# A two-layer hybrid diffusion transformer on one core: the tensor engine keeps the written order of its products and transposes

## The chip, the core and the metric

The kernel runs on one core of a Trainium2 chip. Its time is that of one execution on the device, in microseconds (us). A core has five engines, each with a queue of its own that it works through in order: PE (matrix products and transposes; its loads of stationary operands are shown apart as PEld), DVE (vectors), ACT (scalar functions and copies), POOL (general) and SP, which here only issues DMAs. Products go to PSUM, which is used in eight banks; everything else is in the on-chip memory SBUF.

## The reference

Two layers over 512 tokens (256 of a context, 256 latent), width 1024. All arithmetic is fp32. Per layer, with modulation vectors m that are linear in SiLU of a condition:

```python
h  = rms_norm(x, g) * (1 + scale) + shift            # adaln, per token
x += 0.5 * gate1 * (silu(h @ w_gate) * (h @ w_up)) @ w_down
h  = adaln(x)
x += gate2 * (sum_b sigmoid(h @ G_b + b_b) * (y_b(h) @ w_branch[b])) @ w_out
x += 0.5 * gate3 * swiglu(adaln(x))                   # as in line 2, other weights
```

The four branches y_b of the middle step, the mixer, are a gated short convolution, window attention with a sink, a recurrence run in both directions (RG-LRU), and attention over a neighbourhood on a grid. Context tokens read only context; latent tokens read both. The second layer's mixer and second feed-forward half are needed for the latent tokens alone. The output is the latent stream.

## The kernel before

**Tiling.** The stream lives transposed in eight tiles `x[c]` of 128 features by 512 tokens (columns 0 to 255 context, 256 to 511 latent). An fp32 product is made of three products (`mm3`, L189): high part by high part, high by low, low by high. Weights come from HBM by SP's DMAs (`fetch`, `take`), ACT copies the high part (L150) and DVE subtracts to get the low one (L151). One `mm3` term with 256 columns is three instructions of 0.12 us each on PE.

**Banks.** `BANKS` (L54) gives three PSUM banks to tag A, two to B, one each to C, D and E, eight in all. A tile of a tag takes the bank that was given out longest ago, and its first writer must wait until the last reader of that bank's earlier tile is done.

**A stage and its seam.** A feed-forward half (`ffn`, L420) makes 22 gate and up pairs, then eight tiles of the down product. A tile of the down product, or of the mixer's last product, is added to `x[c]` by DVE (`residual`, L396, the instruction is L399). The last two tiles, c = 6 in bank A and c = 7 in bank B, are made for the context tokens first and then for the latent ones (`finish_stream`, L387). Meanwhile the norm of the next stage is made for the context: squares (ACT), their sum over features on PE (`norm_sum`, L318), then `norm_chain` (L323): DVE scales to `ms` (L326), PE transposes it into bank C (L329), POOL takes the power (L333), PE spreads the result over 128 rows (L337, into D for the context and E for the latent tokens), and `norm_apply` (L343) writes h for eight tiles with two DVE instructions (L351, L353) and one ACT instruction each. So the next stage begins on context tokens while the latent half of the last one is still being added. In the mixer the start is L773 to L788: for each of eight k, one term each of two token-major tiles `T` (bank B), then of two feature-major tiles `F` (bank A). In `ffn` it is L443 to L449: for each k, gate and up terms of two pairs (banks A, B, A, B). There are four such seams:

- M1: first feed-forward half to mixer, layer 0 (at 405 us)
- F1: mixer to second feed-forward half, layer 0 (at 844 us)
- F2: layer 0 to layer 1 (at 1212 us)
- M2: first feed-forward half to mixer, layer 1 (at 1579 us)

**What sets the order.** The program is written in one order, in which a small planner (`later`, `spend`, `until`, L167 to L178) sets side work (norm sums, transposes of heads, gates of the recurrence, attention) between the terms of the big products by a running clock. The framework's scheduler then builds each engine's queue from this program; before the change it lets a ready instruction go ahead of one written earlier when its own model of the times says so. In the mixers the heads are transposed by `flip` (L582: PE L585 into bank E, then an ACT copy L586 out of it), which shares the single bank E with the gates of the recurrence (`gate`, L715: PE L719, ACT L720). `turn` (L644) transposes attention weights in bank C. At the program's start `first_tiles` (L373) interleaves modulation sets (`mod_set`, L259), the first norm, and the first gate and up terms.

Of the kernel before, what the change touches and what calls it, by code (L numbers as in the profile page):

```python
# [35 lines left out]
class Net:  # L36
    def __init__(self, nc, tc, a, out, ctx):
        self.nc, self.tc, self.a, self.out = nc, tc, a, out
        self.n = 0
        pool = lambda name, bufs, **k: ctx.enter_context(tc.tile_pool(name=name, bufs=bufs, **k))  # L40
        self.cp = pool("cst", 1)
        self.hp = pool("h", 16)
        self.wp = pool("w", 3)
        self.whp = pool("wh", 4)
        self.bp = pool("b", 1)
        self.sp = pool("small", 2)
        self.pp = pool("psum", 1, space=PSUM)
# [139 lines left out]


    def mm3(self, ps, wh, wl, xh, xl, first, last):  # L189
        mm = self.nc.tensor.matmul  # L190
        mm(ps, wh, xh, start=first, stop=False)  # L191
        mm(ps, wh, xl, start=False, stop=False)  # L192
        mm(ps, wl, xh, start=False, stop=last)  # L193
# [65 lines left out]
    def mod_set(self, l, s):  # L259
        nc = self.nc  # L260
        ps = self.ps("D", (128, 128))
        for k in range(KC):
            w = self.first[s, k][:].rearrange("p (g n) -> p g n", g=4)
            for g in range(4):
                nc.tensor.matmul(ps[32 * g:32 * g + 32, :], self.sc[:, k, :], w[:, g, :], start=(k == 0),  # L265
                                 stop=(k == KC - 1), tile_position=(0, 32 * g))
        sb = self.half()[:, 0:128]
        nc.scalar.activation(sb, ps, AF.Copy)
        pt = self.ps("E", (128, 4, 32))
        nc.tensor.transpose(pt[:].rearrange("p g n -> p (g n)"), sb, self.ident)  # L270
        bm = self.par[l][:, O_BM + 4 * s:O_BM + 4 * s + 4]
        nc.vector.tensor_tensor(self.mods[l][:, s], pt[:, :, 0:2], bm.unsqueeze(2).to_broadcast([128, 4, 2]), op=ALU.add)
        self.derive(l, s)
# [11 lines left out]
    def norm_stat(self, n, c, s):  # L285
        nc = self.nc
        if c == 0:
            n["ps"][s] = self.ps("DE"[s], (64, 128))
        sq = self.half()
        nc.scalar.activation(sq, self.x[c][:, 256 * s:256 * s + 256], AF.Square)  # L290
        for t in range(2):
            nc.tensor.matmul(n["ps"][s][32 * t:32 * t + 32, :], self.ones, sq[:, 128 * t:128 * t + 128],
                             start=(c == 0), stop=(c == KC - 1), tile_position=(0, 32 * t))

    def norm_square(self, n, c, s):
# [15 lines left out]
    def norm_sum(self, n, s, c, sq):  # L311
        nc = self.nc
        if c == 6:
            n["ps"][s] = self.ps("DE"[s], (64, 128))
        for t in range(2):
            w = slice(128 * t, 128 * t + 128)
            for p, v in enumerate((n["acc"][s], sq) if c == 6 else (sq,)):
                nc.tensor.matmul(n["ps"][s][32 * t:32 * t + 32, :], self.ones, v[:, w], start=(c == 6 and p == 0),  # L318
                                 stop=(c == 7), tile_position=(0, 32 * t))
        if c == 7:  # L320
            self.job(self.norm_chain(n, s), (n["l"], n["i"], s))

    def norm_chain(self, n, s, R=None):  # L323
        nc = self.nc
        ms = self.small((64, 128), "ms", 2)
        nc.vector.tensor_scalar(ms, n["ps"][s], 1.0 / D, EPS, op0=ALU.mult, op1=ALU.add)  # L326
        yield 500
        pt = self.ps("C" if R is None else "A", (128, 2, 32))
        nc.tensor.transpose(pt[:].rearrange("p g n -> p (g n)"), ms, self.ident[:64, :64])  # L329
        v = self.small((128, 2), "v4")  # L330
        nc.vector.tensor_copy(v, pt[:, :, 0])
        r = self.small((128, 2), "r4")
        nc.gpsimd.tensor_tensor(r, v, self.mhalf.to_broadcast([128, 2]), op=ALU.pow)  # L333
        yield 2500 if s else 1900
        n["R"][s] = self.ps("DE"[s], (128, 256)) if R is None else R
        for t in range(2):
            nc.tensor.matmul(n["R"][s][:, 128 * t:128 * t + 128], r[:, t:t + 1].to_broadcast([128, 128]), self.ident,  # L337
                             start=True, stop=True)
        if R is None:
            for c in range(KC):  # L340
                self.norm_apply(n, c, s)
# [225 lines left out]
    def heads(self, ps, t, nh, gain, dst, rot, tag):  # L567
        nc = self.nc
        w = 64 * nh
        q = self.blk(tag, (128, 256))  # L570
        nc.scalar.activation(q[:, :w], ps[:, :w], AF.Copy)
        sq = self.half()
# [4 lines left out]
        r = self.small((128, 4), "rs")  # L577
# [4 lines left out]
        def flip(x, out):  # L582
            pt = self.ps("E", (128, 2, 128))
            for p in range(np_):
                nc.tensor.transpose(pt[:, p], x[:, 128 * p:128 * p + 128], self.ident)  # L585
            nc.scalar.activation(out, pt[:, :np_], AF.Copy)  # L586
            self.pending -= 1

# [55 lines left out]
    def turn(self, p, nk):  # L644
        nc = self.nc
        pt = self.ps("C", (128, 4, 128))
        for j in range(nk // 128):
            nc.tensor.transpose(pt[:, j], p[:, 128 * j:128 * j + 128], self.ident)  # L648
        pT = self.blk("a", (128, 4, 128))
        nc.scalar.activation(pT[:, :nk // 128], pt[:, :nk // 128], AF.Copy)  # L650
        return pT

    def attend(self, step, segs, out, keys, queries, value, biases, sink):


        nc = self.nc
        U = [(pr, sg, qb) for pr in range(2) for sg in segs for qb in range(2)]
        P, T, Y, bias = {}, {}, {}, {}
        nk = lambda u: 512 if u[1] else 256

        def scores(u):
            pr, sg, qb = u
            qw = slice(128 * qb, 128 * qb + 128)
            S = [self.ps("B"), self.ps("B")]
            for j in range(nk(u) // 256):
                for hh in range(2):
                    rows = slice(64 * hh, 64 * hh + 64)
                    nc.tensor.matmul(S[hh][:, 256 * j:256 * j + 256], queries(sg, j)[rows, pr, qw], keys(j, pr)[rows],  # L668
                                     start=True, stop=True)
            P[u] = self.softmax(S, nk(u), (lambda hh: bias[pr](hh, qb)) if sg else None, lambda hh: sink(pr, hh))  # L670
            if pr == 0 and u == U[len(U) // 2 - 1]:
                bias[1] = biases(1)

        def values(u):
            pr, sg, qb = u
            if qb == 0:
                Y[pr, sg] = self.ps("D", (128, 256))
            y = Y[pr, sg]
            n = nk(u) // 128
            for j in range(n):  # L680
                for hh in range(2):
                    nc.tensor.matmul(y[64 * hh:64 * hh + 64, 128 * qb:128 * qb + 128], value(j, pr, hh), T[u, hh][:, j],  # L682
                                     start=(j == 0), stop=(j == n - 1), tile_position=(0, 64 * hh))
            if qb == 1:
                if len(out) == pr:
                    out.append(self.blk("ya"))
                nc.scalar.activation(out[pr][:, 256 * sg:256 * sg + 256], y, AF.Copy)

        bias[0] = biases(0)
        while self.pending:  # L690
            yield 300
        for i in range(len(U) + 2):
            a, b, c = (U[i - d] if 0 <= i - d < len(U) else None for d in range(3))
            if c:
                values(c)
                yield step
            if b:
                T[b, 0] = self.turn(P[b][0], nk(b))
                yield step
            if a:  # L700
                scores(a)
                yield 2 * step
            if b:
                T[b, 1] = self.turn(P.pop(b)[1], nk(b))
            yield 2 * step

    def recurrence(self, segs, out, U, bd, sp2, hb, step):
        nc = self.nc
        S3 = lambda x: x[:].rearrange("p (s t) -> p s t", s=2)
        for c in range(2):  # L710
            for d in range(2):
                k = 2 * d + c
                u = U[c] if d == 0 else U[c][:, ::-1, :]

                def gate(j, g):  # L715
                    pz = self.ps("E")
                    for s in range(2):
                        src = s if d == 0 else 1 - s
                        nc.tensor.matmul(pz[:, 256 * s:256 * s + 256], bd[:, 4 * j + k], U[c][:, src], start=True, stop=True)  # L719
                    nc.scalar.activation(g, pz, AF.Tanh, scale=0.5, bias=hb[:, 4 * j + k:4 * j + k + 1])  # L720

                t, q, b = (self.blk("r") for _ in range(3))
# [7 lines left out]
                w = self.blk("t")  # L730
# [305 lines left out]
```

## Time and profile before

| | |
|---|---|
| median of three runs | 2041.42 us (2040.87 to 2042.23) |
| profiled execution: time, span | 2040.34 us, 2038.6 us |
| PE busy | 2010.8 us, 99% of the span |
| DVE busy, ACT busy | 1331.3 us (65%), 800.3 us (39%) |
| granted clock of PE over the span | 0.997 |
| DMA | 145 GB/s, 41.4% of its engines' time |

An engine's idle time costs only where the chain that ended last runs through it. A row of the timeline gives start, length and, in square brackets, how long the engine had been idle before and what released it. PE's records overlap (a product's record is 0.28 long while the next begins 0.12 later), so the distance of the starts is what a product takes.

### The profile page before, as it was taken

How to read it: one execution, taken by the hardware profiler on the slowest of the kernel's cores; microseconds unless marked ns; L12 is line 12 of the kernel's file. 1: busy time of each engine (PE TensorE's matmuls, PEld its weight loads, DVE VectorE, ACT ScalarE, POOL GpSimd, SP SyncE). 2: the span in 40 equal slices, each digit the busy share in tenths (PEclk: the TensorE clock that was granted, in tenths of full speed). 3: DMA queues.
4: the chain of work that ended last, by engine and by line, in shares of the span. 5: the costliest groups of instructions: out<-in, count | busy, mean ns of one | idle time of the engine just before them, and what ended most of it. 6: DMA issues, size and time to landing. Idle time of an engine off the chain costs nothing.

```text
span 2038.6 us, 29838 instructions
## 1 busy us (share of the span) xinstructions
PE 2010.8 (99%) x11765; PEld 1732.7 (85%) x11765; DVE 1331.3 (65%) x2914; ACT 800.3 (39%) x1311; POOL 87.3 (4%) x90
## 2 busy tenths in 40 slices
PE   7999999999999999999999999999999999999999
PEld 4888887897797788888888888888888999999999
DVE  4878986667555545685733358689844788775554
ACT  3332232356444434232222333222323676664443
POOL 0000000120010000100000010000002101010000
PEclk9999999999999999999999999999999999999999
DMA  9554653522222224244532233446434324463453
GB/s 350 167 212 172 223 207 125 180 68 60 70 91 76 78 94 154 83 166 152 186 106 90 72 139 145 173 168 237 179 125 131 86 91 136 152 231 141 169 191 121
DMA packets 61549, 295.50 MB, mean 145 GB/s; under 512 B 14689, under 2 KB 16353, under 8 KB 38241
## 3 DMA queue, kind: packets, MB, share of 16 engines
q1 hardware_dynamic: 61408, 293.60, 41.4%
q8 instruction: 92, 1.51, 0.3%
q14 instruction: 49, 0.39, 0.1%
HBM read 292.53 MB, written 1.05 MB: 144 GB/s over the span
## 4 chain that ended last, share of the span: by engine, by line
PE 93%; DVE 3%; issue 2%; DMA 1%; ACT 1%; POOL 0%; SPq 0%; POOLq 0%; ACTq 0%; DVEq 0%
PE A L191 19%; PE A L192 18%; PE A L193 18%; PE B L191 11%; PE B L192 11%; PE B L193 11%; DVE a L249 1%; PE B L668 1%; PE D L682 1%; PE C L648 1%; PE E L719 1%; DVE wl L151 1%; DMA w<-in_dn 0%; ACT wh L150 0%; PE D L265 0%
## 5 line engine op out<-in xcount | busy, mean ns | idle before, releaser
L150 ACT ACTIVATE wh<-w 128x1024 fp32r<-128x1024 f32 (+2 forms) x476 | 428.1, 905 | 863.7 <-PE A L192 333.5
L151 DVE TENSOR_TENSOR wl<-w,wh 128x1024 fp32r<-128x1024 f32 (+2 forms) x476 | 490.1, 1033 | 286.5 <-ACT wh L150 283.6
L191 PE MATMUL A<-h,wh 128*128 128x512 f32 (+1 forms) x1440 | 506.9, 352 | 5.8 <-ACT wh L150 3.3
L193 PE MATMUL A<-h,wl 128*128 128x512 f32 (+1 forms) x1440 | 496.2, 345 | 1.2 <-DVE wl L151 1.1
L192 PE MATMUL A<-h,wh 128*128 128x512 f32 (+1 forms) x1440 | 496.3, 345 | 0.7 <-DVE h L353 0.7
L249 DVE CUSTOM_DVE_ANT_0 a<-w,rows 128x512 f32<-128x512 f32 x512 | 350.4, 695 | 41.1 <-DMA w<-in_mod 32.3
L191 PEld LDWEIGHTS A<-h,wh 128*128 128x128 f32 x1440 | 273.2, 190 | 48.3 <-issue 11.5
L193 PEld LDWEIGHTS A<-h,wl 128*128 128x128 f32 x1440 | 273.4, 190 | 35.1 <-DVE wl L151 2.5
L192 PEld LDWEIGHTS A<-h,wh 128*128 128x128 f32 x1440 | 273.5, 190 | 31.8 <-DVE h L353 1.4
L191 PE MATMUL B<-h,wh 128*128 128x512 f32 (+1 forms) x736 | 262.2, 356 | 0.0
L193 PE MATMUL B<-h,wl 128*128 128x512 f32 (+1 forms) x736 | 261.7, 356 | 0.0
L192 PE MATMUL B<-h,wh 128*128 128x512 f32 (+1 forms) x736 | 261.7, 356 | 0.0
L191 PEld LDWEIGHTS B<-h,wh 128*128 128x128 f32 x736 | 139.8, 190 | 19.9 <-ACT wh L150 0.4
L192 PEld LDWEIGHTS B<-h,wh 128*128 128x128 f32 x736 | 139.7, 190 | 19.6 <-issue 0.4
L193 PEld LDWEIGHTS B<-h,wl 128*128 128x128 f32 x736 | 139.6, 190 | 19.6
L432 DVE TENSOR_TENSOR t<-t,B 128x512 f32<-128x512 f32 (+1 forms) x88 | 54.2, 619 | 107.4 <-PE B L193 106.4
L307 POOL TENSOR_TENSOR nb<-nb,l 128x256 f32<-128x256 f32 x45 | 47.2, 1066 | 1320.0 <-ACT l L305 1320.0
L191 PE MATMUL A<-b,wh 128*128 128x512 f32 (+1 forms) x246 | 85.4, 347 | 1.0 <-ACT wh L150 1.0
L193 PE MATMUL A<-b,wl 128*128 128x512 f32 (+1 forms) x246 | 85.1, 346 | 1.1 <-DVE wl L151 1.1
L192 PE MATMUL A<-b,wh 128*128 128x512 f32 (+1 forms) x246 | 84.9, 345 | 0.0
L191 PE MATMUL B<-b,wh 128*128 128x512 f32 (+1 forms) x204 | 73.1, 358 | 0.4 <-ACT wh L150 0.4
L193 PE MATMUL B<-b,wl 128*128 128x512 f32 (+1 forms) x204 | 73.1, 358 | 0.3 <-DVE wl L151 0.3
(266 smaller groups left out, 2927.4 us busy)
## 6 DMA issues: line engine op xcount, KB each, us to landing
w<-in_gu SPq DMA_DIRECT2D x88, 1024.0 KB, 4.9
w<-in_mod SPq DMA_DIRECT2D x64, 1024.0 KB, 4.8
w<-in_dn SPq DMA_DIRECT2D x64, 704.0 KB, 4.1
w<-in_gb SPq DMA_DIRECT2D x64, 640.0 KB, 3.8
w<-in_fm SPq DMA_DIRECT2D x10, 1024.0 KB, 4.8
w<-in_tm SPq DMA_DIRECT2D x10, 1024.0 KB, 5.0
w<-in_wo SPq DMA_DIRECT2D x8, 1024.0 KB, 4.8
b<-in_first SPq DMA_DIRECT2D x20, 256.0 KB, 6.2
```

The lines of the kernel that those rows point to most:

```text
L150: nc.scalar.activation(hi[i][:, :e], t[:, o:o + e], AF.Copy)
L151: nc.vector.tensor_tensor(lo[i][:, :e], t[:, o:o + e], hi[i][:, :e].bitcast(F32), op=ALU.subtract)
L191: mm(ps, wh, xh, start=first, stop=False)
L192: mm(ps, wh, xl, start=False, stop=False)
L193: mm(ps, wl, xh, start=False, stop=last)
L249: nc.vector.tensor_tensor_reduce(out=junk, in0=w[:, g, k], in1=self.rows[:, v, k], scale=1.0, scalar=0.0, op0=ALU.mult, op1=ALU.add, accum ...
L307: nc.gpsimd.tensor_tensor(n["acc"][s], n["acc"][s], sq, op=ALU.add)
L432: nc.vector.tensor_tensor(s[:, lo:hi], s[:, lo:hi], ps[1][:, lo:hi], op=ALU.mult)
L648: nc.tensor.transpose(pt[:, j], p[:, 128 * j:128 * j + 128], self.ident)
L668: nc.tensor.matmul(S[hh][:, 256 * j:256 * j + 256], queries(sg, j)[rows, pr, qw], keys(j, pr)[rows], start=True, stop=True)
L682: nc.tensor.matmul(y[64 * hh:64 * hh + 64, 128 * qb:128 * qb + 128], value(j, pr, hh), T[u, hh][:, j], start=(j == 0), stop=(j == n - 1), ...
L719: nc.tensor.matmul(pz[:, 256 * s:256 * s + 256], bd[:, 4 * j + k], U[c][:, src], start=True, stop=True)
```

## The change

`Net` gets an object `pe` whose `matmul` and `transpose` issue the same instruction and mark it to be kept in the program's order on its engine: no wait is added to the instruction, but the scheduler may no longer let another instruction of PE go ahead of it. All of PE's issues go through it (`mm3`, `mod_set`, `norm_stat`, `norm_sum`, `norm_chain`, `flip`, `turn`, both products in `attend`, `gate`). Shown are the addition and two of the ten places; the others read alike.

```diff
     def __init__(self, nc, tc, a, out, ctx):
         self.nc, self.tc, self.a, self.out = nc, tc, a, out
+        mm, tr = nc.tensor.matmul, nc.tensor.transpose
+        class PEq:
+            pass
+        self.pe = PEq()
+        self.pe.matmul = lambda *a, **k: tc.keep_in_program_order(mm(*a, **k))
+        self.pe.transpose = lambda *a, **k: tc.keep_in_program_order(tr(*a, **k))
...
     def mm3(self, ps, wh, wl, xh, xl, first, last):
-        mm = self.nc.tensor.matmul
+        mm = self.pe.matmul
...
             for p in range(np_):
-                nc.tensor.transpose(pt[:, p], x[:, 128 * p:128 * p + 128], self.ident)
+                self.pe.transpose(pt[:, p], x[:, 128 * p:128 * p + 128], self.ident)
```

The instructions are the same ones. 525 of PE's 11,257 stand in another place, by at most 50 places; so do 176 of DVE's and 36 of ACT's, none of POOL's. All of PE's have the line of one of the two lambdas now (L43 products, L44 transposes), and all later lines of the file move by six (L399 becomes L405).

PE at seam M1, before; B_3365 and B_3366 are the two token-major tiles `T`, A_3363 and A_3364 the feature-major ones, h_294, h_296 the high parts of h for k = 0, 1:

```order
L191 MATMUL B_3365<-wh_3079,h_294 128x256
L192 MATMUL B_3365<-wl_3081,h_294 128x256
L193 MATMUL B_3365<-wh_3079,h_295 128x256
L191 MATMUL A_3363<-h_294,wh_3069 128x256
L192 MATMUL A_3363<-h_295,wh_3069 128x256
L193 MATMUL A_3363<-h_294,wl_3071 128x256
L191 MATMUL A_3364<-h_294,wh_3070 128x256
L192 MATMUL A_3364<-h_295,wh_3070 128x256
L193 MATMUL A_3364<-h_294,wl_3072 128x256
L191 MATMUL B_3365<-wh_3079,h_296 128x256
```

And now:

```order
L43 MATMUL B_3365<-wh_3079,h_294 128x256
L43 MATMUL B_3365<-wl_3081,h_294 128x256
L43 MATMUL B_3365<-wh_3079,h_295 128x256
L43 MATMUL B_3366<-wh_3079,h_294 128x256
L43 MATMUL B_3366<-wl_3081,h_294 128x256
L43 MATMUL B_3366<-wh_3079,h_295 128x256
L43 MATMUL A_3363<-h_294,wh_3069 128x256
L43 MATMUL A_3363<-h_295,wh_3069 128x256
L43 MATMUL A_3363<-h_294,wl_3071 128x256
L43 MATMUL A_3364<-h_294,wh_3070 128x256
L43 MATMUL A_3364<-h_295,wh_3070 128x256
L43 MATMUL A_3364<-h_294,wl_3072 128x256
```

The terms of the second token-major tile B_3366 stood 31 rows after the first row shown; now its first three stand right behind the first three of B_3365, and the products of k = 0 in bank A behind them.

DVE at the same seam, before: the last applications of the context's norm, and between them the residual of the latent half of tile 7 (x_94 from B_3088, the tile whose bank B_3366 takes next):

```order
L351 SCALAR_TENSOR_TENSOR l_3242<-x_93,A_83,D_3215 128x256
L353 SCALAR_TENSOR_TENSOR h_303<-l_3234,mods_81,h_302 128x256
L351 SCALAR_TENSOR_TENSOR l_3246<-x_94,A_83,D_3215 128x256
L353 SCALAR_TENSOR_TENSOR h_305<-l_3238,mods_81,h_304 128x256
L399 SCALAR_TENSOR_TENSOR x_94<-B_3088,G_85,x_94 128x256
L353 SCALAR_TENSOR_TENSOR h_307<-l_3242,mods_81,h_306 128x256
L555 TENSOR_TENSOR nb_4011<-nr_4003,cst 128x256
```

And now:

```order
L357 SCALAR_TENSOR_TENSOR l_3242<-x_93,A_83,D_3215 128x256
L359 SCALAR_TENSOR_TENSOR h_303<-l_3234,mods_81,h_302 128x256
L357 SCALAR_TENSOR_TENSOR l_3246<-x_94,A_83,D_3215 128x256
L359 SCALAR_TENSOR_TENSOR h_305<-l_3238,mods_81,h_304 128x256
L405 SCALAR_TENSOR_TENSOR x_94<-B_3088,G_85,x_94 128x256
L359 SCALAR_TENSOR_TENSOR h_307<-l_3242,mods_81,h_306 128x256
L561 TENSOR_TENSOR nb_4011<-nr_4003,cst 128x256
```

On DVE nothing moved here: the residual has the same place behind the same instructions.

PE at seam F1, before; A_7372, B_7373 are gate and up of the first pair, A_7374, B_7375 of the second:

```order
L191 MATMUL A_7372<-h_3288,wh_7095 128x256
L191 MATMUL B_7373<-h_3288,wh_7096 128x256
L191 MATMUL A_7374<-h_3288,wh_7171 128x256
L192 MATMUL A_7372<-h_3289,wh_7095 128x256
L193 MATMUL A_7372<-h_3288,wl_7097 128x256
L192 MATMUL B_7373<-h_3289,wh_7096 128x256
L193 MATMUL B_7373<-h_3288,wl_7098 128x256
L192 MATMUL A_7374<-h_3289,wh_7171 128x256
L193 MATMUL A_7374<-h_3288,wl_7173 128x256
```

And now:

```order
L43 MATMUL A_7372<-h_3288,wh_7095 128x256
L43 MATMUL A_7372<-h_3289,wh_7095 128x256
L43 MATMUL A_7372<-h_3288,wl_7097 128x256
L43 MATMUL B_7373<-h_3288,wh_7096 128x256
L43 MATMUL B_7373<-h_3289,wh_7096 128x256
L43 MATMUL B_7373<-h_3288,wl_7098 128x256
L43 MATMUL A_7374<-h_3288,wh_7171 128x256
L43 MATMUL A_7374<-h_3289,wh_7171 128x256
L43 MATMUL A_7374<-h_3288,wl_7173 128x256
L43 MATMUL B_7375<-h_3288,wh_7172 128x256
L43 MATMUL B_7375<-h_3289,wh_7172 128x256
L43 MATMUL B_7375<-h_3288,wl_7174 128x256
```

B_7375 stood 43 rows behind the first row shown (and the low-part products behind the high-part ones); now it is the fourth tile to begin.

PE in layer 0's mixer, before; E_3771 is a gate of the recurrence, E_3781 and E_3788 are flips, A_3753 a token-major tile:

```order
L719 MATMUL E_3771<-b_3345,bd_3304 128x256 x2
L191 MATMUL A_3753<-wh_3356,h_304 128x256
L192 MATMUL A_3753<-wl_3358,h_304 128x256
L193 MATMUL A_3753<-wh_3356,h_305 128x256
L191 MATMUL A_3753<-wh_3356,h_306 128x256
L192 MATMUL A_3753<-wl_3358,h_306 128x256
L193 MATMUL A_3753<-wh_3356,h_307 128x256
L191 MATMUL A_3753<-wh_3356,h_308 128x256
L585 MATMUL E_3781<-cst,m_3634 128x128 x2
```

And now:

```order
L43 MATMUL E_3771<-b_3345,bd_3304 128x256 x2
L43 MATMUL A_3753<-wh_3356,h_304 128x256
L43 MATMUL A_3753<-wl_3358,h_304 128x256
L43 MATMUL A_3753<-wh_3356,h_305 128x256
L44 MATMUL E_3781<-cst,m_3634 128x128 x2
L43 MATMUL A_3753<-wh_3356,h_306 128x256
L43 MATMUL A_3753<-wl_3358,h_306 128x256
L43 MATMUL A_3753<-wh_3356,h_307 128x256
L44 MATMUL E_3788<-cst,m_3643 128x128 x2
```

The flip E_3781 comes four products earlier, and E_3788, which stood 21 rows further on, follows three products behind it. The same piece stands in layer 1's mixer with other numbers.

## Rows read from the trace of the kernel before

**Rows 1.** The page: busy time of each engine; the chain's shares by engine.
```profile
PE 2010.8 (99%) x11765; PEld 1732.7 (85%) x11765; DVE 1331.3 (65%) x2914; ACT 800.3 (39%) x1311; POOL 87.3 (4%) x90
...
PE 93%; DVE 3%; issue 2%; DMA 1%; ACT 1%; POOL 0%; SPq 0%; POOLq 0%; ACTq 0%; DVEq 0%
```
**Rows 2.** PE's waits: line, what for, total us, times, longest us.
```profile
PE E L337 <- POOL r L333: 2.5, 5, 1.0
PE A L191 <- ACT h L352: 2.3, 2, 1.2
PE A L193 <- DVE wl L151: 2.1, 4, 0.8
...
PE E L270 <- ACT l L268: 0.9, 2, 0.5
```
**Rows 3.** Timeline of PE, 832 to 835: start, length, instruction, idle before.
```profile
834.07 0.30 PE L318 MATMUL D<-l,ones 128*32 128x128 f32 x1 [1.71 <-ACT l L305]
...
834.63 0.39 PE L191 MATMUL B<-b,ya 128*128 128x256 f32 x1
```
**Rows 4.** Timeline of PE and DVE at seam M1.
```profile
405.75 0.28 PE L191 MATMUL A<-h,wh 128*128 128x256 f32 x1
...
407.98 0.47 DVE L399 SCALAR_TENSOR_TENSOR x<-B,G,x 128x256 f32<-128x256 f32 x1
```
**Rows 5.** Timeline of PE and DVE at seam F1.
```profile
844.93 0.39 PE L192 MATMUL A<-h,wh 128*128 128x256 f32 x1
845.15 0.28 PE L193 MATMUL A<-h,wl 128*128 128x256 f32 x1
...
848.73 0.48 DVE L399 SCALAR_TENSOR_TENSOR x<-B,G,x 128x256 f32<-128x256 f32 x1
...
851.30 0.67 DVE L249 CUSTOM_DVE_ANT_0 a<-w,rows 128x512 f32<-128x512 f32 x1
```
**Rows 6.** Timeline of PE and DVE at seam F2.
```profile
1212.85 0.28 PE L191 MATMUL A<-h,wh 128*128 128x256 f32 x1
...
1214.49 0.47 DVE L399 SCALAR_TENSOR_TENSOR x<-B,G,x 128x256 f32<-128x256 f32 x1
```
**Rows 7.** Timeline of PE and DVE at seam M2.
```profile
1579.22 0.28 PE L191 MATMUL A<-h,wh 128*128 128x256 f32 x1
...
1581.44 0.48 DVE L399 SCALAR_TENSOR_TENSOR x<-B,G,x 128x256 f32<-128x256 f32 x1
```
**Rows 8.** Timeline of ACT and PE in layer 0's mixer.
```profile
440.52 0.69 ACT L720 ACTIVATE r<-E,lr 128x512 f32<-128x512 f32 x1 [1.96 <-PE E L719]
440.67 0.28 PE L191 MATMUL A<-wh,h 128*128 128x256 f32 x1
441.22 1.28 ACT L726 ACT_TABLE_LOAD   x1
441.26 0.44 PE L585 MATMUL E<-cst,m 128*128 128x128 f32 x2
443.24 0.36 ACT L586 ACTIVATE b<-E 128x256 f32<-128x256 f32 x1
450.79 0.41 PE L585 MATMUL E<-cst,m 128*128 128x128 f32 x2 [0.61 <-DVE m L593]
```
**Rows 9.** Timeline of ACT in layer 1's mixer.
```profile
1613.98 0.69 ACT L720 ACTIVATE r<-E,lr 128x512 f32<-128x512 f32 x1 [1.29 <-PE E L719]
...
1616.70 0.36 ACT L586 ACTIVATE b<-E 128x256 f32<-128x256 f32 x1
```
**Rows 10.** Timeline of DVE in layer 0's attention.
```profile
464.92 0.61 DVE L641 TENSOR_SCALAR a<-a,mx 128x256 f32<-128x256 f32 x2
```
**Rows 11.** Windows: stretch, length, each engine's busy time (instructions), clock, DMA share, GB/s.
```profile
832.00:836.00 4.00, 2.29 (x20) 1.83 (x20) 2.10 (x5) 0.42 (x1) 0.55 (x1) 1.00 0.80 289
1838.40:1843.50 5.10, 1.47 (x10) 0.80 (x9) 1.94 (x6) 0.92 (x3) 0.71 (x1) 0.97 0.02 6
1843.50:1847.00 3.50, 3.44 (x17) 3.44 (x18) 3.50 (x10) 2.40 (x7) 0.00 (x0) 0.55 0.00 0
1847.00:1851.00 4.00, 4.00 (x35) 4.00 (x35) 1.87 (x5) 0.95 (x2) 0.00 (x0) 1.00 0.00 0
```

More of the change, by code (lines that the diff above doesn't have):

```diff
@@ L264, in mod_set @@
             for g in range(4):
-                nc.tensor.matmul(ps[32 * g:32 * g + 32, :], self.sc[:, k, :], w[:, g, :], start=(k == 0),
+                self.pe.matmul(ps[32 * g:32 * g + 32, :], self.sc[:, k, :], w[:, g, :], start=(k == 0),
                                  stop=(k == KC - 1), tile_position=(0, 32 * g))
@@ L269, in mod_set @@
         pt = self.ps("E", (128, 4, 32))
-        nc.tensor.transpose(pt[:].rearrange("p g n -> p (g n)"), sb, self.ident)
+        self.pe.transpose(pt[:].rearrange("p g n -> p (g n)"), sb, self.ident)
         bm = self.par[l][:, O_BM + 4 * s:O_BM + 4 * s + 4]
@@ L291, in norm_stat @@
         for t in range(2):
-            nc.tensor.matmul(n["ps"][s][32 * t:32 * t + 32, :], self.ones, sq[:, 128 * t:128 * t + 128],
+            self.pe.matmul(n["ps"][s][32 * t:32 * t + 32, :], self.ones, sq[:, 128 * t:128 * t + 128],
                              start=(c == 0), stop=(c == KC - 1), tile_position=(0, 32 * t))
@@ L317, in norm_sum @@
             for p, v in enumerate((n["acc"][s], sq) if c == 6 else (sq,)):
-                nc.tensor.matmul(n["ps"][s][32 * t:32 * t + 32, :], self.ones, v[:, w], start=(c == 6 and p == 0),
+                self.pe.matmul(n["ps"][s][32 * t:32 * t + 32, :], self.ones, v[:, w], start=(c == 6 and p == 0),
                                  stop=(c == 7), tile_position=(0, 32 * t))
@@ L328, in norm_chain @@
         pt = self.ps("C" if R is None else "A", (128, 2, 32))
-        nc.tensor.transpose(pt[:].rearrange("p g n -> p (g n)"), ms, self.ident[:64, :64])
+        self.pe.transpose(pt[:].rearrange("p g n -> p (g n)"), ms, self.ident[:64, :64])
         v = self.small((128, 2), "v4")
@@ L336, in norm_chain @@
         for t in range(2):
-            nc.tensor.matmul(n["R"][s][:, 128 * t:128 * t + 128], r[:, t:t + 1].to_broadcast([128, 128]), self.ident,
+            self.pe.matmul(n["R"][s][:, 128 * t:128 * t + 128], r[:, t:t + 1].to_broadcast([128, 128]), self.ident,
                              start=True, stop=True)
@@ L647, in turn @@
         for j in range(nk // 128):
-            nc.tensor.transpose(pt[:, j], p[:, 128 * j:128 * j + 128], self.ident)
+            self.pe.transpose(pt[:, j], p[:, 128 * j:128 * j + 128], self.ident)
         pT = self.blk("a", (128, 4, 128))
@@ L667, in scores @@
                     rows = slice(64 * hh, 64 * hh + 64)
-                    nc.tensor.matmul(S[hh][:, 256 * j:256 * j + 256], queries(sg, j)[rows, pr, qw], keys(j, pr)[rows],
+                    self.pe.matmul(S[hh][:, 256 * j:256 * j + 256], queries(sg, j)[rows, pr, qw], keys(j, pr)[rows],
                                      start=True, stop=True)
@@ L681, in values @@
                 for hh in range(2):
-                    nc.tensor.matmul(y[64 * hh:64 * hh + 64, 128 * qb:128 * qb + 128], value(j, pr, hh), T[u, hh][:, j],
+                    self.pe.matmul(y[64 * hh:64 * hh + 64, 128 * qb:128 * qb + 128], value(j, pr, hh), T[u, hh][:, j],
                                      start=(j == 0), stop=(j == n - 1), tile_position=(0, 64 * hh))
@@ L718, in gate @@
                         src = s if d == 0 else 1 - s
-                        nc.tensor.matmul(pz[:, 256 * s:256 * s + 256], bd[:, 4 * j + k], U[c][:, src], start=True, stop=True)
+                        self.pe.matmul(pz[:, 256 * s:256 * s + 256], bd[:, 4 * j + k], U[c][:, src], start=True, stop=True)
                     nc.scalar.activation(g, pz, AF.Tanh, scale=0.5, bias=hb[:, 4 * j + k:4 * j + k + 1])
```

## Prediction

> **What bounds the kernel now.** I read the page's busy times and chain first: PE is busy 99% of the span, and 93% of the chain that ended last runs through it [rows 1]. So neither bandwidth nor another engine sets the time; it is the sum of PE's products plus the little that PE stands still. The busy figure leaves 2038.6 − 2010.8 = 27.8 us, some 12 of it before the first product. The work on PE is the same after the change, product for product, so the question is only what idle time a new order adds to these 28 us or takes from them. The list of PE's waits shows what there is to take: in the running part single waits of at most a few tenths each [rows 2]. Then I compared the old and new order of PE and, wherever an instruction comes earlier, asked of the timeline when the thing it needs is there. Where it is ready before PE arrives, the move costs nothing; where not, everything behind it stands, since PE has nothing else in its queue that could go ahead. That this is so, the trace shows: PE stood 1.71 us for one square sum (L318) while the product that came right behind, L191 into B, had all its data [rows 3].
>
> **The four seams.** At M1 the first three products of B_3366 now stand right after those of B_3365. PE reached that place at 405.75 [rows 4]: the product that starts there is the one which stood next in the old order. The bank of B_3366 is that of tile 7 of the down product, of which DVE has yet to read the latent half. On DVE the residual stands behind the context's norm applications and has not moved; it starts at 407.98 and lasts 0.47 [rows 4]. A hand-over from another engine to PE took 0.05 (ACT's copy of 440.52 + 0.69 ends at 441.21, the transpose that waited for it starts at 441.26) [rows 8]. So PE starts B_3366 at 408.50 and stands 408.50 − 405.75 = 2.75. Before, 31 other instructions stood between and hid it.
>
> At F1 the second product of all needs a low part that DVE delivers for 844.93; the third follows at 845.15 [rows 5], and six more come at 0.12 each, so that the tenth, the first of B_7375, is due at 845.15 + 7 × 0.12 = 845.99. The residual ends at 848.73 + 0.48 = 849.21 [rows 5], with the hand-over 849.26: a wait of 3.27. At F2 the fourth tile is due at 1212.85 and free at 1214.49 + 0.47 + 0.05 = 1215.01: 2.16 [rows 6]. At M2 it is 1579.22 against 1581.44 + 0.48 + 0.05 = 1581.97: 2.75 [rows 7]. The four make 10.93.
>
> Behind each of these waits the context's chain goes on without PE, so that the latent norm is helped: the waits of L337 for POOL's power (2.5 in 5, of which 1.0 is in the start [rows 2]) go, −1.5. F1 pays twice more: two products that filled the gap before 844.93 come later (2 × 0.12 = 0.24), and one more background product of DVE, 0.67 long and followed by a short read [rows 5], gets ahead of `ms`; it costs between 0 and 0.75, and I take 0.55, since DVE is idle for some tenths there. Seams: 10.93 + 0.8 − 1.5 = 10.2. What else waits behind: nothing on DVE or ACT is short of time, as they run 65% and 39% [rows 1].
>
> **The flips.** E_3781 comes four products earlier, at 440.67, right behind three products that follow a gate in the same bank. ACT has read the gate at 441.21, so the flip still starts at 441.26 [rows 8]: 0.59 that four products used to fill. E_3788 then follows three products behind it, at about 441.26 + 0.27 + 3 × 0.12 = 441.89, and needs bank E back. The copy that frees it stands on ACT behind a table load of 1.28 and an exponential; it starts at 443.24 and ends at 443.60 [rows 8]. With 0.05 for the hand-over, 443.65 − 441.89 = 1.76. Since the heads go on earlier, the wait of 0.61 at 450.79 [rows 8] goes. Layer 1 has the same piece, with the copy 2.72 after the gate's reading starts in both (443.24 − 440.52, 1616.70 − 1613.98) [rows 8, 9]: 0.59 + 1.76 again, and there no later wait to save. Flips: 2 × 2.35 − 0.61 = 4.1.
>
> **Single moves.** Some six more instructions (turns of attention weights in both layers, the start of the last stage on latent tokens alone) come a few products earlier than their data. Each is then ended by one DVE or ACT instruction under way, at most 0.6 long [rows 10]: between 0 and 3.6, and I take half, 1.8.
>
> **The start.** Up to 61 us the order changes most, but there PE waits for weights and h anyway. The two waits for h (2.3) may go [rows 2]; against that, the transposes of the modulation sets wait 0.45 each for ACT's copy in two of four steps, and with nothing let in between they do in all four, 2 × 0.45 = +0.9 [rows 2]. Bounds −2.3 and +0.9; I take −1.0, a little below the middle, as the next sets no longer break into the gate and up products.
>
> **The clock.** A stall has a second price if it lowers PE's clock. In the trace 1.71 us of standing did not: the granted clock of 832 to 836 is 1.00 (2.4 GHz). A stretch of 5.10 us with 1.47 of work did: the 3.5 us behind it ran at 0.55, near the lower level of 1.2 GHz, with 17 products in 3.44, against 35 in 4.00 after that [rows 11]. Such a fall costs 3.44 − 17 × 4.00 / 35 = 1.5. The new stalls of 2.2 to 3.3 lie between the two cases; I take one fall for the four, 1.5, with bounds 0 and 6.0.
>
> **Sum.** 10.2 + 4.1 + 1.8 − 1.0 + 1.5 = 16.6 on the profiled execution's 2040.34: 2056.9. The median shown is 1.1 above that execution, so 2058.
>
> **The rivals.** First, *the clock falls at all four seams*: 3 × 1.5 more, 2062.5. For it speaks the 1838 stretch, against it that PE is full up to each stall and from its end on. The Trainium skill ("TensorE: Matmul & The Clock Gate", Part 1: The HAM clock gate) has it that the array drops to half rate once it has been idle and comes back only after a spell of sustained work; by that rule this would be the case to expect for the longest stalls, and the 832 window disagrees only for one that is shorter. Chance 0.15.
>
> Second, on the other side, *the residual doesn't hold the bank*: the new tile lands in the bank of tile 5's, read long before (two banks of B are given out in turn, so this turns on one tile more or less), or PE lets the ready products past. Then the seams cost nothing and the savings stay, and the flips, whose copies come in a stream, shrink to the singles: 2041.4 − 1.5 − 0.6 − 1.0 + 1.8 = 2040, not slower. It decides from the point that the residual ends before 405.75, 2.7 us earlier than it does. Against it: the residual is the tile's last reader and stands right there in DVE's queue [rows 4], and PE did not let a ready product past [rows 3]. Chance 0.08.
>
> Third, *part is given back later*: an engine that has been ahead catches up less work later, so that some of PE's old waits vanish, for low parts of weights (2.1 [rows 2]) and for square sums such as the 1.71 [rows 3], with a few singles absent, together about 6 us: 2052. Against it: those waits are set by DMAs and by products just before them, which a late PE delays too. Chance 0.07.
>
> **How the numbers follow.** Forecast 0.70, rivals 0.15, 0.08, 0.07. The lower bounds of the sum (F1's 0.55, singles and clock 0, start −2.3) give 2058 − 0.55 − 1.8 − 1.5 − 1.3 = 2053, the third rival reaches a little lower, so the range begins at 2050; the upper ones (singles +1.8, start +1.9, clock +4.5) give 2066, where it ends. About what a measurement of this kernel can tell from no change is 0.2%, 4.1 us: the forecast and the first and third rivals are slower by more, 0.92; the second lies mostly within it, 0.06, and 0.02 is left for faster.
>
> **What would show it.** Right: four waits of PE on DVE's residual (now L405) of 2 to 3.3 us at 405, 845, 1212 and 1580 (plus what has been added before), two of 1.8 us on ACT's copy out of E in the mixers, the four waits at the latent L337 gone, PE's idle time up from 28 to about 43 us and its busy time unchanged but for the clock. Wrong: no row of PE waiting for a residual; a clock of 1.00 through all seams (the term of 1.5 falls) or about 0.5 behind each (the first rival); an idle time that is far above 45 us.

## The result, and the profile after

The changed kernel takes 2063.48 us (2060.78 to 2066.44, four runs) against 2041.26 us (2040.87 to 2042.23, four runs): a ratio of 1.0108, interval 1.0096 to 1.012, so 22.2 us slower. The forecast was 2058, the range 2050 to 2066. The profiled execution took 2063.92 us, its span is 2062.1 us. PE's busy time, in the page:

```profile
PE 2017.6 (98%) x11765; PEld 1743.4 (85%) x11765; DVE 1332.1 (65%) x2914; ACT 800.2 (39%) x1311; POOL 87.0 (4%) x90
```

As many instructions as before [rows 1] (the 11,257 in the section on the change is not the page's count), but 6.8 us more of busy time. That is a net figure: some 4.6 less in the start and about 11 more where PE ran at half clock, as will be seen. The rest of the 23.5 us by which the span grew is idle time of PE. Its waits (line, what for, total us, times, longest us):

```profile
PE B L43 <- DVE x L405: 10.3, 4, 3.1
...
PE E L44 <- ACT b L592: 3.2, 2, 1.6
...
PE E L44 <- ACT r L726: 0.9, 2, 0.4
PE B L43 <- ACT m L577: 0.8, 2, 0.4
```

The first line is the four seams, which were in no line before. The next two are the flips: E_3788 and its like wait for ACT's copy, E_3781 for its reading of the gate. Of the five waits for POOL's power at L337 [rows 2] the one of the last stage is left; the four at the seams are gone. M1 and the layer-0 flip in the timeline:

```profile
405.47 0.47 DVE L405 SCALAR_TENSOR_TENSOR x<-B,G,x 128x256 f32<-128x256 f32 x1
...
406.00 0.39 PE L43 MATMUL B<-wh,h 128*128 128x256 f32 x1 [2.59 <-DVE x L405]
...
446.64 0.36 ACT L592 ACTIVATE b<-E 128x256 f32<-128x256 f32 x1
...
447.05 0.44 PE L44 MATMUL E<-cst,m 128*128 128x128 f32 x2 [1.60 <-ACT b L592]
```

The residual ends at 405.94 and PE goes on 0.06 later, as it was worked out from [rows 4, 8]. Then the clock (windows: stretch, length, busy time of each engine with its instructions, granted clock, DMA share, GB/s):

```profile
408.00:412.00 4.00, 4.00 (x17) 3.66 (x18) 0.39 (x2) 0.00 (x0) 0.70 (x1) 0.50 0.36 28
...
416.00:420.00 4.00, 4.00 (x36) 4.00 (x35) 4.00 (x12) 2.36 (x6) 0.00 (x0) 1.00 0.00 1
...
840.60:844.00 3.40, 3.40 (x19) 3.40 (x18) 0.48 (x1) 0.42 (x1) 0.00 (x0) 0.52 0.76 294
855.00:859.00 4.00, 2.87 (x13) 2.26 (x13) 3.96 (x13) 0.97 (x3) 0.00 (x0) 0.50 0.00 0
1224.00:1228.00 4.00, 1.99 (x16) 1.45 (x16) 4.00 (x12) 2.24 (x5) 0.00 (x0) 1.00 0.30 125
1228.00:1232.00 4.00, 4.00 (x32) 3.80 (x33) 0.66 (x3) 0.00 (x0) 0.70 (x1) 1.00 0.71 260
1595.50:1599.50 4.00, 3.96 (x18) 3.35 (x19) 1.73 (x5) 0.42 (x1) 0.00 (x0) 0.50 0.12 10
```

Behind M1, F1 and M2 PE ran at the lower level, 1.2 GHz, with 17 or 18 products in 4 us where 36 is the full rate (at F1 13 in 2.87 us of work); behind F2 (2.0 us of standing) it did not. And the old stall of 1.71 us, which did nothing to the clock before [rows 11], has a fall behind it now, at 840.60.

Where the 23.5 us of span are, from where the same instruction stands in the two traces, and from the idle times in each stretch:

| stretch | longer by | of it, PE standing | rest |
|---|---|---|---|
| start, to 352 us | −1.8 | | |
| M1 and mixer, layer 0 | +7.2 | 4.4 | 2.8 |
| F1, with the stall ahead of it | +6.6 | 3.0 | 3.6 |
| F2 | +1.6 | 1.7 | 0 |
| M2 and mixer, layer 1 | +8.5 | 5.2 | 3.3 |
| last stage | +1.4 | 0.2 | 1.2 |

The rest is put down to the clock. Counted the other way, product by product at half clock against the mean of its shape at full clock, the five stretches give 3.2, 4.1, 0, 3.2 and 1.3, so about 11 by either count. The start's −1.8 holds for these two executions only: the kernels that share the changed kernel's start reach their 151st product of 512 columns at 69.2 to 73.4 us, the kernel before reached it at 72.4 in its one trace.

### The profile page after: what moved, and what is told of

Its sections match the earlier page's. It is cut to its first block, busy times and chain, and to the rows that moved or that the text cites. A ratio compares the mean times of both kernels' runs of the same rounds, so it can differ in the third digit from the quotient of the medians.

```text
span 2062.1 us, 29832 instructions
## 1 busy us (share of the span) xinstructions
PE 2017.6 (98%) x11765; PEld 1743.4 (85%) x11765; DVE 1332.1 (65%) x2914; ACT 800.2 (39%) x1311; POOL 87.0 (4%) x90
## 5 line engine op out<-in xcount | busy, mean ns | idle before, releaser
L43 PE MATMUL A<-h,wh 128*128 128x512 f32 (+1 forms) x2880 | 754.6, 350 | 6.4 <-ACT wh L156 3.3
L43 PEld LDWEIGHTS A<-h,wh 128*128 128x128 f32 x2880 | 499.7, 191 | 80.3 <-issue 11.1
L43 PE MATMUL A<-h,wl 128*128 128x512 f32 (+1 forms) x1440 | 497.4, 345 | 1.1 <-DVE wl L157 1.1
L43 PE MATMUL B<-h,wh 128*128 128x512 f32 (+1 forms) x1472 | 398.5, 357 | 5.1 <-DVE x L405 5.1
L43 PEld LDWEIGHTS A<-h,wl 128*128 128x128 f32 x1440 | 274.8, 191 | 35.2 <-DVE wl L157 2.7
L43 PEld LDWEIGHTS B<-h,wh 128*128 128x128 f32 x1472 | 263.2, 191 | 44.4 <-DVE x L405 5.5
L43 PE MATMUL B<-h,wl 128*128 128x512 f32 (+1 forms) x736 | 262.2, 356 | 0.0
L43 PEld LDWEIGHTS B<-h,wl 128*128 128x128 f32 x736 | 140.4, 191 | 19.6 <-DVE wl L157 0.2
L43 PE MATMUL A<-b,wh 128*128 128x512 f32 (+1 forms) x492 | 126.6, 346 | 1.3 <-ACT wh L156 1.3
L43 PE MATMUL B<-b,wh 128*128 128x512 f32 (+1 forms) x408 | 110.8, 358 | 0.6 <-ACT wh L156 0.6
L43 PEld LDWEIGHTS A<-b,wh 128*128 128x128 f32 x492 | 85.9, 189 | 13.7 <-ACT wh L156 1.7
L43 PE MATMUL A<-wh,h 128*128 128x256 f32 x448 | 86.4, 288 | 0.0
L43 PE MATMUL A<-b,wl 128*128 128x512 f32 (+1 forms) x246 | 85.0, 345 | 0.5 <-DVE wl L157 0.5
L43 PEld LDWEIGHTS B<-b,wh 128*128 128x128 f32 x408 | 72.7, 189 | 12.2 <-ACT wh L156 1.1
L43 PE MATMUL B<-b,wl 128*128 128x512 f32 (+1 forms) x204 | 73.1, 358 | 0.3 <-DVE wl L157 0.3
L43 PE MATMUL A<-m,wh 128*128 128x512 f32 (+1 forms) x280 | 72.8, 348 | 0.0
L43 PEld LDWEIGHTS A<-wh,h 128*128 128x128 f32 x448 | 71.5, 191 | 0.2
```

The costliest lines, as they stand in the source:

```text
L43: self.pe.matmul = lambda *a, **k: tc.keep_in_program_order(mm(*a, **k))
```

## The experiments

Two questions were open: whether the residual, by way of the bank, is what holds the seams up, and whether the clock falls because PE stands.

**The waiting tile in another bank.**

```diff
-            P = [(self.ps("A"), self.ps("B")) for _ in W]
+            P = [(self.ps("A"), self.ps("A" if m and (l, i) != (0, 0) else "B")) for m in range(len(W))]
-            T = [self.ps("B", (128, 256)), self.ps("B", (128, 256))]
+            T = [self.ps("B", (128, 256)), self.ps("B" if sg else "A", (128, 256))]
```

> The changed kernel, with the tile that waits at each of the four seams put into bank tag A (its third bank, that of tile 6, whose residual DVE does before the norm applications) and no longer into B; order of PE unchanged. If the residual holds the bank, as forecast: the four waits of PE on the residual (10.3 us in all in the changed kernel's list of waits) go, and with them the half-clock stretches behind M1, F1 and M2 (some 7 us): 2063.5 - 10.3 - 7 = 2046, between 2043 and 2050. Rival, that the residual is only the name of the wait and the order around the seams costs the time (low parts, less mixing of tiles): 2058 or more, with other waits in the same places.

Measured: 2062.63 us, ratio 1.0104 (1.009 to 1.0117). The waits for the residual are gone, the time is not. Its list of waits, and M1 in its timeline:

```profile
PE E L43 <- ACT l L311: 10.6, 5, 3.3
```
```profile
406.81 0.42 ACT L311 ACTIVATE l<-x 128x256 f32<-128x256 f32 x1 [0.34 <-DVE x L405]
...
407.28 0.41 PE L43 MATMUL E<-l,ones 128*32 128x128 f32 x4 [2.02 <-ACT l L311]
```

PE now runs on to the square sum of the latent norm, written nine products further, and stands there for ACT's square, which waits for the same residual. In the changed kernel PE comes there so late that the square is done, so this second waiter shows no wait. (In F1 and F2 the shifted turn of bank A also added 4.2 us of waits for `act`.) So the bank is not the only thing that holds PE to the residual. (The time stays about the same although waits were added, since the half-clock stretches of this trace are shorter.)

**Tile later, sum later, both.** The two edits of the next three kernels:

```diff
-            self.later(1100, lambda: self.norm_sum(n, s, c, sq))
+            self.later(4400 if s and len(n["segs"]) == 2 else 1100, lambda: self.norm_sum(n, s, c, sq))
```
```diff
+                late = [(0, 0), (0, 1), (1, 0)] if W[1:] and r == CTX else None
...
-                    for w, ps in zip(W, P):
-                        for j in range(2):
-                            self.term(ps[j], w, 1024 * j, H, *r, k)
+                    for g, j in late or [(g, j) for g in range(len(W)) for j in range(2)]:
+                        self.term(P[g][j], W[g], 1024 * j, H, *r, k)
+                if late:
+                    self.project(P[1][1], W[1], 1024, H, *r)
...
-                for j in range(2):
+                for j in range(1 if sg == 0 else 2):
                     self.token_term(T[j], wt, H, 2 * sg + j, k)
...
+            if sg == 0:
+                for k in range(KC):
+                    self.token_term(T[1], wt, H, 1, k)
```

Tile later alone:

> The changed kernel, with the second token-major tile (mixers) and the fourth gate-and-up tile (feed-forward halves) written behind the other three for the context tokens, so that no product needs the bank before DVE's residual is done; the square sums of the latent norm stay where they were written, some 12 products into the seam. Theory: one residual has two waiters on PE, the bank and, through ACT's square of the same tile, the square sum; the second takes over when the first is gone, as with the tile in the other bank: waits of 2.0, 3.3, 2.2 and 2.0 at the square sum, 2061 (2059 to 2064). Rival: with the tile in the other bank the sum waited only because of the other bank; here it doesn't, 2046 to 2052.

Measured: 2059.83 us, ratio 1.0089 (1.0075 to 1.0103). The waits at the sum are 2.02, 3.26, 2.16 and 2.02, as with the other bank; with the 1.08 of the last stage they make its line:

```profile
PE E L43 <- ACT l L311: 10.6, 5, 3.3
```

The time is 3.6 less than the changed kernel's. In its trace the half-clock stretches at M1 and F1 are half as long and M2 and the stall at 840 have none, while two short ones have come behind the flips.

Sum later alone:

> The changed kernel, with the latent norm's square sums of tiles 6 and 7 due 4400 in place of 1100 of the planner's units later, so that some 30 more products stand ahead of them; tiles and banks as in the changed kernel. Theory of two waiters: the bank's wait of 10.3 us in four stays, nothing gained: 2063 (2060 to 2066). Rival, that the sum is what counts: 2046 to 2055.

Measured: 2068.28 us, ratio 1.0131 (1.0116 to 1.0147): 4.8 slower than the changed kernel, outside what was expected. The wait for the bank stays, and a late latent norm has a price of its own. Timeline, layer 0's mixer:

```profile
406.11 0.38 PE L43 MATMUL B<-wh,h 128*128 128x256 f32 x1 [3.34 <-DVE x L405]
...
427.57 0.74 PE L43 MATMUL B<-wh,h 128*128 128x256 f32 x2 [1.50 <-DVE h L359]
```

PE reaches the bank earlier by the products of the sum and waits for it longer (12.0 in the four seams in place of 10.3), and then waits for the latent tokens' h (1.50 in each mixer): together 4.7 more, close to the 4.8 by which the time grew.

Both:

> The changed kernel with both edits: the tile written behind the other three, and the square sums of the latent norm due 4400 units later. Theory of two waiters: only now the four waits go, 10.3 us, and the half-clock stretches at M1, F1 and M2 with them, some 8 us; the short waits for POOL's power at the latent norm may come back (1.5): 2063.5 - 10.3 - 8 + 1.5 = 2047 (2043 to 2051). Rival: a third waiter behind, 2055 or more.

Measured: 2048.52 us, ratio 1.0032 (1.002 to 1.0045). No wait on the residual is left at the seams, and there is no fall of the clock at M1, F1, F2 or M2. Windows at M1 and F1:

```profile
409.00:413.00 4.00, 4.00 (x34) 3.53 (x32) 2.31 (x7) 0.74 (x2) 0.00 (x0) 1.00 0.13 14
854.00:858.00 4.00, 4.00 (x33) 3.52 (x32) 3.14 (x11) 0.00 (x0) 1.08 (x1) 1.00 0.02 4
```

It takes 15.0 us less than the changed kernel, where either edit alone gave 3.6 and −4.8. So the four seams are a matter of one late residual with two waiters. Two waits for the low part of h remain (1.21 each, in the mixers), the price of the later sum.

**Two banks for the heads' transposes.**

```diff
-            pt = self.ps("E", (128, 2, 128))
+            pt = self.ps("EC"[t % 2], (128, 2, 128))
```

In the changed kernel, with nothing else:

> The changed kernel, with the transposes of the heads in banks E and C in turn and nothing else: the two waits of 1.6 us on ACT's copy go, those at the seams and their half-clock stretches stay: 2063.5 - 3.2 = 2060.3 (2058 to 2063). Rival, that these waits only cover others (ACT's table load delays what comes next anyway): 2062 or more, with waits elsewhere in the mixers.

Measured: 2058.13 us, ratio 1.0083 (1.0069 to 1.0097), 5.3 less than the changed kernel. The line of 3.2 us is gone, the 0.43 for the gate stays, and so does the seams' 10.3. The 2 us beyond 3.2 lie within the spread of the two kernels' runs; in this trace the fall behind the old stall of 1.71 is absent too (granted clock 1.00 from 840.90 to 844.30), which is worth 1.4. With the two edits of before:

> As the kernel with both edits, and the transposes of the heads take bank E and bank C in turn (C is free there), so that the second of two no longer waits for ACT's copy of the first. The waits of 1.6 us in each mixer go and the 0.4 for the gate's reading stay: 3.2 us less than the kernel with both edits, 4 or 5 less if the clock fell behind these waits there; about 2043 (2039 to 2047). Rival: bank C is held too, or the wait moves to the third transpose: no gain.

Measured: 2042.57 us, ratio 1.0004 (0.9995 to 1.0013): what the pinned order lost is given back by writing the program in another order and using a free bank. And with the sum 1000 units sooner:

> As the kernel with the later tile, the later sum and two banks for the head transposes, with the latent norm's square sums due 3400 in place of 4400 units later: 9 instructions of PE earlier, when DVE's residual and ACT's square are just done. The waits for the low part of h in the two mixers (1.2 each) should shrink to about 0.2: 2042.6 - 2 = 2040.6 (2038 to 2043). If instead the sum then waits for ACT's square: 2042 to 2046, with the clock falling again at M1 or M2.

Measured: 2037.9 us, ratio 0.9985 (0.9976 to 0.9994), faster than the kernel before and the changed one, and just below what was expected; the two waits of 1.2 are gone.

**The start alone.** The written order is kept only until the first tiles are done (`self.pin = False` behind `first_tiles`, which both lambdas ask).

> The kernel before, with the written order kept only up to the end of the first gate and up tiles (61 us); all later instructions stand on every engine as before. If the start gains what the two traces show between them (the wait at 353.7 us before comes at 351.9 after): 2041.3 - 1.8 = 2039.5. Rival, that this gain hangs on the later order or on the place of the clock's changes: 2041.3, no change.

Measured: 2039.04 us, ratio 0.999 (0.9981 to 0.9999). From 376 us on every wait has its old size and stands 1.7 to 1.9 earlier, as here the one of the latent norm at M1, 412.59 in the kernel before:

```profile
410.80 0.71 PE L45 MATMUL E<-cst,r 128*128 128x128 f32 x4 [0.35 <-POOL r L341]
```

**Work where PE stood.** `fill` writes products into bank C, which nobody reads: 20 in the mixers, 22 at F1, 15 at F2, ahead of the tile that waits.

```diff
+    def fill(self, w, x, n):
+        ps = self.ps("C", (128, 256))
+        for _ in range(n):
+            self.pe.matmul(ps, w, x, start=True, stop=True)
...
+                    if k == 0 and sg == 0 and j:
+                        self.fill(H[0][0][:, 0:128], wt[0][0][:, 0:256], 20)
                     self.token_term(T[j], wt, H, 2 * sg + j, k)
```

> The changed kernel, with 15 to 22 products of 256 columns, into bank C and read by nobody, written ahead of the tile that waits at each of the four seams, so that PE works (20 x 0.12 = 2.4 us) where it stood; the tile begins no earlier. If the clock falls because PE stands: granted clock 1.00 in the 12 us behind M1, F1 and M2, and 2063.5 - 7 = 2056.5 (2053 to 2060), although no wait is saved. Rival, that these falls have another cause than the standing (thin work over the whole seam, or the place of the seam in time): same time as the changed kernel, 2061 to 2066, with the falls still there.

Measured: 2058.74 us, ratio 1.0084 (1.007 to 1.0098): 4.7 less, with 77 products more. M1 in its timeline, and the clock there:

```profile
405.26 2.56 PE L43 MATMUL C<-wh,h 128*128 128x256 f32 x20
408.02 0.39 PE L43 MATMUL B<-wh,h 128*128 128x256 f32 x1 [0.20 <-DVE x L405]
```
```profile
404.00:408.00 4.00, 3.82 (x32) 3.61 (x31) 4.00 (x12) 2.62 (x6) 0.00 (x0) 1.00 0.58 240
408.00:412.00 4.00, 3.98 (x30) 3.45 (x31) 1.87 (x6) 0.42 (x1) 0.70 (x1) 1.00 0.14 10
```

The tile begins as long after its place as in the changed kernel, and the clock is 1.00 at all four seams. That the falls come from standing there is shown; that they cost all of the 9.7 us in the table's middle rows is not: this kernel saved half of it, and has short half-clock stretches in other places, at 354, 447 and 1631 us, the last two behind the flips' waits of 1.6.

**Stalls by the dose.** In layer 0's second feed-forward half PE is made to wait 16 times for a chain of powers on POOL:

```diff
+    def stall(self, n):
...
+        self.pe.transpose(pt[:].rearrange("p g n -> p (g n)"), self.cst[0:64, 0:128], self.ident[:64, :64])
+        nc.vector.tensor_copy(v, pt[:, :, 0])
+        for _ in range(n):
+            r = self.small((128, 2), "r4")
+            nc.gpsimd.tensor_tensor(r, v, self.ones[:, 0:1].to_broadcast([128, 2]), op=ALU.pow)
+            v = r
...
+        self.pe.matmul(R[:, 0:128], v[:, 0:1].to_broadcast([128, 128]), self.ident, start=True, stop=True)
```

> The changed kernel, with 16 stalls written into the gate and up tiles of layer 0's second feed-forward half, 11 us and more apart: PE transposes a constant, DVE copies, POOL does 1, 2, 3 or 4 powers in a chain (0.71 us each), PE multiplies the result. PE should stand about 1.4, 2.1, 2.8 and 3.5 us, four times each, 39 us in all. If standing of the seams' length lowers the clock: most stalls of 2.8 and 3.5 and few of 1.4 are followed by a stretch at half clock, eight falls or more at 2 to 3.4 us each: about 2063.5 + 39 + 24 = 2127. Rival, that a single stall in full work doesn't lower it: clock 1.00 throughout that half, 2063.5 + 39 = 2102.

Measured, one run: 2136.64 us, 10 above the forecast. PE stood 44.0 us in all, 5 more than forecast; the rest was not taken apart. Windows of 4 us from the end of a stall of 1.02, 2.58, 3.36, 2.10 and 2.87 us:

```profile
918.99:922.99 4.00, 4.00 (x19) 3.33 (x20) 3.90 (x9) 0.45 (x1) 0.00 (x0) 1.00 0.58 240
933.18:937.18 4.00, 4.00 (x12) 3.33 (x13) 3.79 (x12) 0.00 (x0) 0.00 (x0) 0.62 0.26 109
...
949.55:953.55 4.00, 4.00 (x12) 3.19 (x13) 3.49 (x10) 0.00 (x0) 0.00 (x0) 0.57 0.06 27
...
995.19:999.19 4.00, 4.00 (x19) 3.35 (x20) 0.00 (x0) 0.00 (x0) 0.00 (x0) 1.00 0.01 4
...
1009.66:1013.66 4.00, 4.00 (x19) 3.34 (x19) 0.00 (x0) 0.00 (x0) 0.00 (x0) 1.00 0.00 0
```

None of the four stalls of 1.0 to 1.1 us lowered the clock; of the twelve of 2.1 to 4.7 ten did, and the two that didn't are of 2.10 and 2.87. A stretch of half clock lasted 3.4 us, or 6.8 after two of those above 4; at half rate that loses at most 1.7 or 3.4. A lone stall in dense work is enough.

## Why the prediction was right, and what it got wrong

**Seams: right in place and size, incomplete in the cause.** Forecast 10.93 of waits, measured 10.3; 0.8 for F1's side effects, measured 0.3; 1.5 given back by POOL's power, measured 1.4. So 9.2 for 10.2. (The wait of 1.0 for POOL that the text places in the start stands in the last stage, at 1841.67 of the trace before; the 1.5 doesn't depend on it.) The second rival, that the residual doesn't hold the bank, is refuted by the list of waits. But the text took the bank for the only waiter; the square sum behind it would have cost nearly the same (9.5 in the kernel with the other bank), and undoing only the bank would have been a wrong remedy.

**Flips.** Forecast 4.1, measured 2 × (0.43 + 1.60) − 0.61 + 0.19 = 3.6; the wait at 450.79 came back as 0.19.

**Single moves.** 1.8 against 1.4 (two waits of T's banks for the heads' first copy, 0.41 each, and four small ones).

**The start: right in sign, wrong in the reckoning.** −1.0 against −1.8. A row was misread: the 2.3 of waits for h are not both of the start [rows 2], one of 1.18 stands in the last stage, before and after. The other, 1.12, became 1.35. The 0.9 for the modulation sets came as forecast, and the wait of 0.72 at 57.53 went, but two of 1.03 for POOL came that the sum had not: up to 62 us PE stands 14.8 in place of 12.3. (Nor are the waits behind the start all "a few tenths", as the text has it: 1.71, 0.99 and 0.81 are among them.) So the gain is not in waits at all. It is in the work, which the text names only as an aside ("the next sets no longer break into the gate and up products"). 12 to 62 us before, then after:

```profile
12.00:62.00 50.00, 43.19 (x375) 27.85 (x376) 26.19 (x81) 16.85 (x29) 2.37 (x3) 0.93 0.80 302
12.00:62.00 50.00, 41.14 (x392) 30.87 (x387) 29.89 (x89) 19.89 (x33) 2.41 (x3) 0.93 0.86 331
```

More products in less busy time, at the same clock: 32 modulation products in one piece take 0.89 (36.81 to 37.70), where a piece of 8 took 0.36 (28.14 to 28.50 before), and a gate or up product of the start takes 0.24 on average at full clock in place of 0.26. What the start gains is best taken from the runs of the kernel that pins it alone: 2.3 us less, with an interval of 0.2 to 3.9.

**The clock: the step that failed.** "One fall for the four, 1.5", with bounds of 0 and 6.0, measured about 11 (the table's last column): falls behind three of the four seams, one behind the old stall of 1.71, and a longer one in the last stage. This is the first rival, which had a chance of 0.15, in three places of four; its price was wrong too, with 2.8 and 3.3 for the falls at M1 and M2 in place of 1.5, since the one fall read in the trace of before was a short one. The rule cited from the Trainium skill ("TensorE: Matmul & The Clock Gate", Part 1: The HAM clock gate), that an idle array drops to half rate, agrees with the chip here at M1, with 17 products in 4 us behind 2.59 of standing, and not at F2, where nothing fell behind 2.01. The weight given to the 832 window was too great, for the same stall of 1.71 has a fall behind it in one trace and none in the other. The sum of the other terms, 15.1 forecast, is 12.4 in the measured ones, so two errors of opposite sign kept the time within the range. That was luck: with the clock's 10.9 and the other terms as forecast the time would be 2067, outside it. Of the third rival nothing is seen: the waits for weights at 351 to 372 us shrank and grew by a few tenths, and later none has shrunk but POOL's and the flip's, which were counted.

**Left open.** Which stall lowers the clock is settled only as a matter of odds: F2 in the changed kernel has none behind 2.01 us, the same seam in the kernel with 16 stalls has one, and 2.87 us in full work had none. All twelve traces together, without the start and the last stage, show how the odds go with the length of the stall: about two in five up to 2.2 us, nearly all from 2.4 us on, a fall being counted when it began in the stall or within 2 us of its end:

| PE stood, us | stalls | with a fall |
|---|---|---|
| 1.5 to 1.8 | 28 | 11 |
| 2.0 to 2.2 | 11 | 4 |
| 2.4 to 4.7 | 26 | 25 |

So the prediction's 1.71 without a fall was the commoner outcome of such a stall, and three of the four new stalls were of a length behind which a fall came in all cases but one. The changed kernel's four runs spread over 5.7 us, with the granted clock lowest in the slowest (0.990 at 2066.44, 0.993 at 2060.78). The kernel before spreads over 1.4 in its four runs, but over 3.1 to 4.7 in sets of 15, so that differences of 2 us between kernels of four runs each say little.

## What to carry to other kernels

Before an order is pinned, look for the first instruction that each late result holds up, and then for the second: an edit that frees the first alone may give nothing, and here only both together gave 15 us. Count a stall of two microseconds or more on a full tensor engine at more than its length, since it may be paid again in clock (here in all but one of 26 cases from 2.4 us on). Pin where the scheduler's guesses lose (here the start, where its order broke the modulation sets into small pieces) and rewrite the order, or leave it free, where they win.

## What had not been expected of the hardware

A single stall of 2.1 to 4.7 us in dense work was followed by half clock in 10 cases of 12, for 3.4 or 6.8 us. Work that nobody reads can be worth its place there: 77 such products made the changed kernel 4.7 us faster.
